# A state space layer's opening: two vectors spread over the partitions by TensorE, a shorter rotation, a written order for two engines

## The chip, the core and the metric

The kernel runs on one core of a Trainium2 chip as one program. The metric is the time of the whole program in device microseconds; lower is better. The core's engines are named as the profile names them: PE (TensorE, matmuls; PEld its weight loads), DVE (VectorE), ACT (ScalarE), POOL (GpSimd) and SP (SyncE, which here only issues DMAs).

## What is computed

Two layers of a trunk on a sequence of 512 tokens of width 1024. The first is a diagonal complex state space layer and a feed-forward layer, the second an attention layer and a feed-forward layer. The change lies in the state space layer alone:

```
h = rmsnorm(x, norm_mix[0])                      # gain of 1024 values
lam = complex(lam_re, lam_im)                    # 64 groups x 64 states
dt = exp(log_dt)[:, None]
a_bar = exp(lam * dt)
b_bar = ((a_bar - 1) / lam)[..., None] * complex(b_re, b_im)
bu = einsum('blgh,gph->blgp', h in groups of 16, b_bar)
states = associative_scan(a*, bu)                # over the 512 tokens
y = einsum('blgp,ghp->blgh', states, c).real + d_skip * h
y = gelu(y); val, gate = split(y @ w_glu); out = val * sigmoid(gate)
```

## The kernel before, in words

Everything named here is in `s5`. The 64 groups go in 8 units (`UN`) of 8 groups. Before the loop over the units there is an **opening** that prepares what all units share.

- Loads, all from SP's queue in the order written: `lam`, `ldt`, `braw` (the two parts of b), `xc` (the tokens, 8 loads of 256 KB), `gb`, `craw` (c) and `Dd`. `gb` (L418) is the norm gain, 1024 values, read once for each of 128 partitions. `Dd` (L425) is the skip vector, read for 32 partitions. Behind them come the weights of the GLU, `w_raw` (L262), through a pool of two buffers: a third `w_raw` is not issued before `w_lo` of the first has been computed.
- `wblock` splits each weight block in two: ACT copies `w_raw` to `w_hi` (L263), DVE subtracts to get `w_lo` (L265).
- ACT squares the tokens (`junk`, L457) and sums each row into `ss`. DVE scales `ss` (L491), POOL raises it to the power -1/2 (`rj`, L493). ACT multiplies the tokens by `rj` into `xn` (`normal`, L579; 32 copies for all eight columns), PE transposes them, ACT copies them to `U` (`tokens`, L596).
- b is transposed by PE, copied by ACT (L465), multiplied by `gb` in halves of 64 partitions by DVE (L468), then summed and subtracted (`Bs`, `Bd`, L494 and L495).
- `dt`, its exponential and cosine and sine are chains of DVE instructions on 128x32 elements (`Small`). `input_powers` builds the powers of the input side (`qt`, `qs`); `rotation` squares a phase eight times (`ephr`, `ephi`). `braid` writes the two alternately.
- `tables(u)` builds the table `W` of a unit (five DVE instructions), `turned` transposes it (`WT`, copied by ACT), `lags` and `chunk_inputs` are matmuls with it. `turn_factors` doubles the table `FG` three times with the phases (L699 to L701); `turns(u)` makes `E` of it. `powers` and `output_powers` do the output side. `output_side_out` copies c twice (`Cst`, and swapped `Csw`, ACT L573).

In the loop a unit's `scan` gives `X` on DVE (L750), PE multiplies it (`outputs`, L777 and L778), ACT applies the GELU, and the result `y` feeds the GLU's matmuls (L272 to L274), which `filler` places between the units. After the loop come the rest of the GLU, the feed-forward layer and the attention layer.

No order is written by hand in the opening or the loop (`manual` is an empty stack). The framework's scheduler sets the order of each engine's instructions by its own estimates; each engine then runs its list in that order. DMAs on SP's queue use eight semaphores in turn, so one waits for the eighth before it.

## Time and profile before

| | us |
|---|---|
| three runs | 1294.7, 1295.48, 1298.88 |
| median | 1295.48 |
| the profiled execution | 1299.89 |
| its span in the profile | 1298.2 |

| engine | busy us | share |
|---|---|---|
| PE | 1223.8 | 94% |
| DVE | 769.0 | 59% |
| ACT | 541.9 | 42% |
| POOL | 150.5 | 12% |

The shares are means over stages of different kinds. In the page's 40 slices of 32.5 us, PE's digits begin 2 5 6 9 and stay at 9, with one 8, while DVE's begin 7 9 9 9 9: the opening and the first units are the only stretch in which PE is not full. The span and what lies around it (1.7 us) make the profiled execution's own time; it stands 4.4 us above the median of the three runs. Times in the trace count from the span's start. An instruction's duration in the timeline overlaps the next one's by about 0.1 us, so the distance from start to start is what an engine's list costs.

### The profile page before, as it was taken

The page shows a single profiled execution, that of the slowest core. Times are in us where ns is not written, and L with a number is a line of the kernel's source. Part 1 is how long each engine was busy: PE and PEld are TensorE (multiplying, and loading weights), DVE is VectorE, ACT ScalarE, POOL GpSimd, SP SyncE. Part 2 cuts the span into 40 slices and gives each one's busy share as a digit, 9 for nine tenths or more (in the row PEclk, how much of TensorE's full clock was granted, in tenths as well). Part 3 has the DMA queues.
Part 4 walks back from the last instruction along what each step waited for, and adds up shares of the span by engine and source line. Part 5 has one row for each costly group of instructions (what it writes and reads, how often), then busy time and mean ns, then how long its engine had stood idle before and what let it go on. Part 6 is the DMA issues. An engine that isn't in the chain of part 4 may idle for free.

```text
span 1298.2 us, 17961 instructions
## 1 busy us (share of the span) xinstructions
PE 1223.8 (94%) x6796; PEld 1048.7 (81%) x6796; DVE 769.0 (59%) x1546; ACT 541.9 (42%) x1224; POOL 150.5 (12%) x177
## 2 busy tenths in 40 slices
PE   2569999999999999999989799999999999999998
PEld 1457878888888888888989799998888888888887
DVE  7999958654444443335899977775754444443221
ACT  5645536433333322223563678875533333332221
POOL 2000000000000000005744354520000000000000
PEclk9979999999999999999999899999999999999999
DMA  5101223333333333332213111111333333333341
GB/s 139 54 19 52 71 84 114 104 98 97 97 98 98 98 92 99 94 105 71 92 52 98 49 50 34 42 30 53 106 112 95 96 96 95 97 93 101 108 118 46
DMA packets 189894, 108.65 MB, mean 84 GB/s; under 512 B 7224, under 2 KB 188560, under 8 KB 189744
## 3 DMA queue, kind: packets, MB, share of 16 engines
q1 hardware_dynamic: 189424, 107.35, 28.4%
q8 instruction: 53, 0.87, 0.3%
q14 instruction: 33, 0.27, 0.1%
q10 hardware_dynamic: 384, 0.16, 0.1%
HBM read 103.04 MB, written 2.10 MB: 81 GB/s over the span
## 4 chain that ended last, share of the span: by engine, by line
PE 75%; DVE 8%; ACT 1%; issue 1%; DMA 0%; POOL 0%; ACTq 0%; DVEq 0%; POOLq 0%
PE acc L272 21%; PE acc L273 21%; PE acc L274 21%; PE acc L1026 7%; PE acc L1231 2%; DVE mask L1134 2%; DVE m L1133 2%; PE tr L1220 1%; DVE mask L1121 1%; PE lg L1204 1%; DVE pe L1207 1%; PE lg L1203 1%; PE tr L1063 0%; DVE kl L1081 0%; ACT pe L1210 0%
## 5 line engine op out<-in xcount | busy, mean ns | idle before, releaser
L263 ACT ACTIVATE w_hi<-w_raw 128x1024 fp32r<-128x1024 f32 (+5 forms) x208 | 199.9, 963 | 508.2 <-PE acc L273 461.1
L265 DVE TENSOR_TENSOR w_lo<-w_raw,w_hi 128x1024 fp32r<-128x1024 f32 (+6 forms) x179 | 194.2, 1085 | 146.5 <-ACT w_hi L263 145.4
L272 PE MATMUL acc<-h,w_hi 128*128 128x512 f32 x704 | 274.5, 390 | 0.0
L274 PE MATMUL acc<-h,w_lo 128*128 128x512 f32 x704 | 273.9, 389 | 0.0
L273 PE MATMUL acc<-h,w_hi 128*128 128x512 f32 x704 | 273.7, 389 | 0.0
L1026 PE MATMUL acc<-w_hi,h 128*128 128x256 f32 (+1 forms) x896 | 175.6, 293 | 0.8 <-ACT h L284 0.8
L272 PEld LDWEIGHTS acc<-h,w_hi 128*128 128x128 f32 x704 | 132.1, 188 | 28.0 <-issue 0.5
L274 PEld LDWEIGHTS acc<-h,w_lo 128*128 128x128 f32 x704 | 132.1, 188 | 27.6
L273 PEld LDWEIGHTS acc<-h,w_hi 128*128 128x128 f32 x704 | 132.1, 188 | 27.5 <-issue 0.5
L1026 PEld LDWEIGHTS acc<-w_hi,h 128*128 128x128 f32 x896 | 142.1, 193 | 1.4 <-ACT h L284 1.0
L1026 PE MATMUL acc<-w_lo,h 128*128 128x256 f32 (+1 forms) x448 | 127.3, 289 | 0.3 <-POOL w_lo L267 0.3
L339 DVE TENSOR_TENSOR u<-acc,rinv 128x512 f32<-128x512 f32 x44 | 30.4, 691 | 132.4 <-PE acc L274 132.4
L272 PE MATMUL acc<-f,w_hi 128*128 128x512 f32 x272 | 106.4, 391 | 0.0
L274 PE MATMUL acc<-f,w_lo 128*128 128x512 f32 x272 | 105.9, 389 | 0.0
L273 PE MATMUL acc<-f,w_hi 128*128 128x512 f32 x272 | 105.8, 389 | 0.0
L1026 PEld LDWEIGHTS acc<-w_lo,h 128*128 128x128 f32 x448 | 85.5, 193 | 0.8 <-POOL w_lo L267 0.5
L336 DVE TENSOR_TENSOR g<-acc,rinv 128x512 f32<-128x512 f32 x44 | 30.4, 691 | 85.3 <-PE acc L274 85.1
L267 POOL TENSOR_TENSOR w_lo<-w_raw,w_hi 128x1024 fp32r<-128x1024 f32 (+2 forms) x29 | 69.5, 2407 | 47.6 <-ACT w_hi L263 46.8
L274 PEld LDWEIGHTS acc<-f,w_lo 128*128 128x128 f32 x272 | 51.0, 188 | 10.8
L273 PEld LDWEIGHTS acc<-f,w_hi 128*128 128x128 f32 x272 | 51.1, 188 | 10.4
L272 PEld LDWEIGHTS acc<-f,w_hi 128*128 128x128 f32 x272 | 51.1, 188 | 10.4
L272 PE MATMUL acc<-y,w_hi 128*128 128x512 f32 x128 | 51.9, 414 | 1.7 <-ACT y L796 1.1
(288 smaller groups left out, 1979.4 us busy)
## 6 DMA issues: line engine op xcount, KB each, us to landing
w_raw<-in_ffn_w_gate_up_dram SPq DMA_DIRECT2D x88, 512.0 KB, 3.7
w_raw<-in_ffn_w_down_dram SPq DMA_DIRECT2D x32, 448.0 KB, 3.5
w_raw<-in_dsa_w_in_dram SPq DMA_DIRECT2D x26, 512.0 KB, 3.4
w_raw<-in_ffn_w_down_dram SPq DMA_DIRECT2D x16, 512.0 KB, 3.7
w_raw<-in_dsa_w_o_dram SPq DMA_DIRECT2D x16, 256.0 KB, 2.9
w_raw<-in_s_w_glu_dram SPq DMA_DIRECT2D x6, 384.0 KB, 3.3
xc<-in_x_dram SPq DMA_DIRECT2D x8, 256.0 KB, 8.9
xr<-in_x_dram SPq DMA_DIRECT2D x4, 512.0 KB, 3.7
```

Source lines behind the costliest of these rows:

```text
L263: nc.scalar.activation(hi, raw, AF.Copy)
L265: nc.vector.tensor_tensor(lo, raw, hi, op=ALU.subtract)
L267: lo_engine.tensor_tensor(lo, raw, hi, op=ALU.subtract)
L272: mm(out, lhsT=whi, rhs=xx[:, 0], start=start, stop=False)
L273: mm(out, lhsT=whi, rhs=xx[:, 1], start=False, stop=False)
L274: mm(out, lhsT=wlo, rhs=xx[:, 0], start=False, stop=stop)
L336: nc.vector.tensor_tensor(g, ps[0], rinv, op=ALU.mult)
L339: nc.vector.tensor_tensor(u, ps[1], rinv, op=ALU.mult)
L1026: PE.matmul(pt[:, :n], lhsT=h[k][:, l, ts], rhs=ww, start=(k == 0 and i == 0), stop=(k == KT - 1 and i == 2))
L1133: V.max(m8, sc)
L1134: V.match_replace(out=sc, in_to_replace=m8, in_values=sc, imm_value=GONE)
L1231: PE.matmul(po[s, b][:, i * HD : (i + 1) * HD], lhsT=pT[:, j * P : (j + 1) * P], rhs=vv[j][:, (s * 4 + i) * HD : (s * 4 + i + 1) * HD], st ...
```

## The change

Four things change, all in `s5`.

1. **Gain and skip.** `gd`, 8 partitions x 128, holds both vectors (two loads of 4 KB, L414 and L415). `sel`, made by POOL, holds eight selection matrices. PE spreads the gain over the partitions by 16 matmuls (`pgb`), and ACT copies it to `gb`, now 128x512 with each half of the partitions holding its own groups. DVE multiplies skip and gain on 8 partitions (L466), PE spreads the product in 8 matmuls, and ACT copies it to `Dd` in two pieces. The two broadcast loads go, and so does DVE's product on 32x1024. The products with b read the transposes in PSUM directly, on all 128 partitions at once: two DVE instructions and no ACT copy, instead of four and two.
2. **The rotation's layout.** `ephr` and `ephi` are laid out so that `turn_factors` handles both of its parts in one instruction; its first doubling becomes two ACT copies.
3. **A written order.** From `sgn` to the end of the opening the DVE and ACT instructions that are written there keep the order of the code (`manual_schedule`). Instructions written later, in the loop, may still be placed between them; POOL, PE and SP are not bound.
4. **The order of the code.** `dt` moves ahead of the products with b, `Bs` and `Bd` right behind them. Only eight steps of `rotation` are braided with `input_powers`; the rest comes behind the first table. `turn_factors`, `turns` and `powers` move behind the first `lags`, `chunk_inputs`, the copies of c and the tokens.

```
+        gd = self.scratch(1, [KT, 2, P], "gd")
+        nc.sync.dma_start(out=gd[:, 0], in_=gain_row.rearrange("(k p) -> k p", p=P))
+        nc.sync.dma_start(out=gd[:, 1], in_=d_ap.rearrange("(k p) -> k p", p=P))
...
-        nc.sync.dma_start(out=gb.rearrange("p a b c -> p (a b c)"),
-                          in_=gain_row.rearrange("(o d) -> o d", o=1).to_broadcast([P, D]))
...
-        nc.sync.dma_start(out=Dd[DR:], in_=d_ap.rearrange("(o d) -> o d", o=1).to_broadcast([32, D]))
+        sel = self.scratch(0, [KT, KT, SP], "sel")
+        PL.memset(sel, 1.0)
+        PL.affine_select(out=sel, in_=sel, compare_op=ALU.is_equal, fill=0.0, base=0,
+                         pattern=[[-1, KT], [0, SP]], channel_multiplier=1)
+        manual.enter_context(tc.manual_schedule(engines={E_.DVE, E_.Activation}))
...
+        for q in range(KT):
+            for g2 in range(2):
+                PE.matmul(pgb[g2 * SP : (g2 + 1) * SP, q * SP : (q + 1) * SP], lhsT=sel[:, q], rhs=gv[:, :, g2],
+                          start=True, stop=True)
+        AC.activation(gb.rearrange("p a b -> p (a b)"), pgb, AF.Copy)
+        V.tensor_tensor(gd[:, 1], gd[:, 1], gd[:, 0], op=ALU.mult)
+        for half in range(2):
+            pd = self.acc()
+            for q in range(KT // 2):
+                PE.matmul(pd[SP:, q * P : (q + 1) * P], lhsT=sel[:, half * (KT // 2) + q], rhs=gd[:, 1],
+                          start=True, stop=True)
+            AC.activation(Dd[DR:, half * S : (half + 1) * S], pd[DR:], AF.Copy)
...
-            AC.activation(t, pb.rearrange("p (h g) -> p g h", h=H16), AF.Copy)
-            for g2 in range(2):
-                hs = slice(g2 * SP, (g2 + 1) * SP)
-                V.tensor_tensor(t[hs], t[hs], gb[hs, :, g2], op=ALU.mult)
+            V.tensor_tensor(t, pb.rearrange("p (h g) -> p g h", h=H16), gb, op=ALU.mult)
+        V.tensor_tensor(Bs, Br, bi, op=ALU.add)
+        V.tensor_tensor(Bd, bi, Br, op=ALU.subtract)
...
-        braid(input_powers(), rotation())
+        rot = rotation()
+        braid(input_powers(), (next(rot, None) for _ in range(8)))
...
-            for i in range(3):
+            F = FG.rearrange("p j w g n -> p j (w g) n")
+            AC.activation(F[:, 0, :, 1], ephr[:, 0].rearrange("p w g -> p (w g)"), AF.Copy)
+            AC.activation(F[:, 1, :, 1], ephi[:, 0, 1].rearrange("p w g -> p (w g)"), AF.Copy)
+            for i in range(1, 3):
...
+                V.tensor_tensor(f1, F[:, :, :, :n], mr, op=ALU.mult)
+                V.tensor_tensor(f2, F[:, ::-1, :, :n], mi, op=ALU.mult)
+                V.tensor_tensor(F[:, :, :, n : 2 * n], f1, f2, op=ALU.add)
...
+        normal(0)
         for q in range(2):
             output_side_out(q, pc[q], Cst, False)
-        normal(0)
         tokens(0)
         spread(0)
         W = {0: tables(0)}
-        turn_factors()
-        E = {0: turns(0)}
-        powers()
-        V.tensor_tensor(Dd[DR:], Dd[DR:], gb[DR:].rearrange("p a b c -> p (a b c)"), op=ALU.mult)
-        warm_up("w")
         WT = turned(W[0])
         pk = lags(0, W[0])
         S4 = {0: chunk_inputs(0, WT)}
-        ES = {0: turns_out(0, E[0])}
-        output_powers()
+        normal(1)
         for q in range(2):
             output_side_out(q, pc[q], Csw, True)
-        W[1] = tables(1)
+        for _ in rot:
+            pass
+        turn_factors()
+        E = {0: turns(0)}
+        ES = {0: turns_out(0, E[0])}
+        powers()
+        output_powers()
         lags_out(0, pk)
-        VV = readout(0)
-        normal(1)
         tokens(1)
         spread(1)
         normal(2)
+        W[1] = tables(1)
+        VV = readout(0)
+        manual.close()
```

How the engines' lists come out at three places follows. On ACT, behind the squares of the tokens, the list before was this (`Cz` and `RT` are small tables of the first unit):

```order
L457 ACTIVATE junk,ss<-xc_117 128x1024
L579 ACTIVATE xn_376<-xc_114,rj 128x8x16
...
L666 ACTIVATE Cz_140<-Cst 64x4x16 x4
L579 ACTIVATE xn_377<-xc_116,rj 128x8x16
L579 ACTIVATE xn_377<-xc_117,rj 128x8x16
L724 ACTIVATE RT<-r_106 128x4x63
L263 ACTIVATE w_hi<-w_raw 128x512
L263 ACTIVATE w_hi<-w_raw 128x768
```

And in the changed kernel, at the same place:

```order
L479 ACTIVATE junk,ss<-xc_117 128x1024
L263 ACTIVATE w_hi<-w_raw 128x512
L263 ACTIVATE w_hi<-w_raw 128x768 x2
L599 ACTIVATE xn_392<-xc_114,rj 128x8x16
L599 ACTIVATE xn_392<-xc_115,rj 128x8x16
```

The three `w_hi` copies of the GLU's first weights, of which two came behind 20 of the `xn` copies and the third behind all 32, now stand ahead of all of them.

On DVE in the changed kernel the matching `w_lo` subtractions stand inside the chain of small instructions (`sm`, `ks`, `cs`) that leads to the first power and to `ss`; this is the third of them:

```order
L122 SCALAR_TENSOR_TENSOR ks<-sm_295,sm_283 128x32
L122 SCALAR_TENSOR_TENSOR sm_298<-sm_298,sm_292 128x32
L265 TENSOR_TENSOR w_lo<-w_raw,w_hi 128x768
L115 TENSOR_SCALAR ks<-sm_298 128x32
L115 TENSOR_SCALAR sm_277<-sm_301 128x32
```

The first two `w_lo` stand 22 and 15 rows ahead of the third; before, all three came behind the first table `W`. Behind the third the list goes on for 15 rows to the scaling of `ss`, and for 45 more to the end of the first `W`.

The third place is ACT's list around the first column of `FG` in the changed kernel:

```order
L668 ACTIVATE WT<-tr 128x512 x2
...
L599 ACTIVATE xn_392<-xc_117,rj 128x8x16
L593 ACTIVATE Csw<-acc_394,sgn 64x512 x2
L593 ACTIVATE Csw<-acc_399,sgn 64x512 x2
L712 ACTIVATE FG<-ephr 128x64
L713 ACTIVATE FG<-ephi 128x64
```

and DVE's list where that column is read:

```order
L659 TENSOR_TENSOR W<-k_426,k_431 128x512
L122 SCALAR_TENSOR_TENSOR ephi<-ephr,ephi 128x32
...
L721 TENSOR_TENSOR f_502<-FG,ephr 128x128x2
L722 TENSOR_TENSOR f_503<-FG,ephi 128x128x2
L723 TENSOR_TENSOR FG<-f_502,f_503 128x128x2
```

Between the first `xn` copy and the first `FG` copy ACT's list holds 27 more `xn` copies, eight copies of c, four of `U`, four of `Cz`, one of `RT` and two of `WT`. Between the end of the first `W` and its first reading of `FG`, DVE's list holds 17 rows of the rotation. Before, `FG`'s first column came from DVE itself.

## Rows read from the trace of the kernel before

**Rows 1.** Two stretches of 20 us: length, busy us (and instructions) of each engine, TensorE's granted clock, DMA share, GB/s.

```profile
60.00:80.00 20.00, 13.71 (x119) 11.68 (x118) 19.51 (x38) 8.34 (x22) 0.12 (x1) 0.83 0.07 16
...
140.00:160.00 20.00, 20.00 (x157) 16.59 (x155) 19.35 (x35) 10.15 (x19) 0.11 (x1) 1.00 0.27 79
```

**Rows 2.** Timeline of the opening up to `rj`: start, duration, engine, line, operation, count, and in brackets the idle time before it and who ended it.

```profile
12.77 1.39 DVE L468 TENSOR_TENSOR hB<-hB,gb 64x512 f32<-64x512 f32 x2 [3.52 <-DMA gb<-in_norm_mix_dram]
...
14.36 1.38 DVE L468 TENSOR_TENSOR bi<-bi,gb 64x512 f32<-64x512 f32 x2
...
18.82 1.06 ACT L457 ACTIVATE junk<-xc 128x1024 f32<-128x1024 f32 x1 [1.15 <-DMA xc<-in_x_dram]
...
20.00 0.17 DVE L491 TENSOR_SCALAR ss<-ss 128x4 f32<-128x4 f32 x1 [0.96 <-ACT junk L457]
...
20.25 1.09 POOL L493 TENSOR_TENSOR rj<-ss,mhalf 128x4 f32<-128x4 f32 x1 [14.94 <-DVE sm L100]
```

**Rows 3.** The DMA view of the first 30 us: busy tenths in 40 slices of 0.75 us, the sum of the bytes, and two loads with their KB and us from issue to landing.

```profile
DMA  0001769999889999999999995797720000000000
...
DMA packets 3873, 4.51 MB, mean 150 GB/s; under 512 B 2408, under 2 KB 3136, under 8 KB 3808
...
gb<-in_norm_mix_dram SPq DMA_DIRECT2D x1, 512.0 KB, 8.2
w_raw<-in_s_w_glu_dram SPq DMA_DIRECT2D x1, 384.0 KB, 4.3
```

**Rows 4.** The tile `w_raw` in the first 60 us: line, engine, operation, count, duration in ns (least, median, most), first and last start; and the time of its loads from issue to landing.

```profile
L263 ACT ACTIVATE w_hi<-w_raw x3: 613/827/845, 37.2 to 46.0; 128x768 fp32r<-128x768 f32 x2, 128x512 fp32r<-128x512 f32 x1
L265 DVE TENSOR_TENSOR w_lo<-w_raw,w_hi x3: 691/946/951, 37.8 to 48.4; 128x768 fp32r<-128x768 f32 x2, 128x512 fp32r<-128x512 f32 x1
...
DMA to landing us min/median/max: 3.0/3.7/4.3
```

**Rows 5.** ACT's timeline from 20 to 48 us.

```profile
21.38 5.07 ACT L579 ACTIVATE xn<-xc,rj 128x128 f32<-128x128 f32 x17 [1.42 <-POOL rj L493]
26.36 1.37 ACT L573 ACTIVATE Cst<-acc,sgn 64x512 f32<-64x512 f32 x2
...
30.26 1.54 ACT L596 ACTIVATE U<-tr 64x256 f32<-64x256 f32 x4
...
36.87 0.40 ACT L724 ACTIVATE RT<-r 128x252 f32<-128x252 f32 x1
...
41.76 0.60 ACT L648 ACTIVATE WT<-tr 128x512 f32<-128x512 f32 x1
...
46.78 1.04 ACT L666 ACTIVATE Cz<-Cst 64x64 f32<-64x64 f32 x4
```

**Rows 6.** DVE's timeline: two small instructions, the last of the first `W` and the one behind it, and `FG` from its first instruction to the first of `turns`.

```profile
27.30 0.17 DVE L117 TENSOR_SCALAR ephr<-sm 128x32 f32<-128x32 f32 x1
27.39 0.18 DVE L100 TENSOR_TENSOR sm<-ephi 128x32 f32<-128x32 f32 x1
...
36.07 0.68 DVE L639 TENSOR_TENSOR W<-k,k 128x512 f32<-128x512 f32 x1
36.67 0.21 DVE L606 TENSOR_TENSOR t<-pwt,pow 128x64 f32<-128x64 f32 x1
...
38.42 0.27 DVE L699 TENSOR_TENSOR f<-FG,ephr 128x64 f32<-128x64 f32 x1
...
44.09 0.42 DVE L712 TENSOR_TENSOR e<-FG 128x256 f32<-128x256 f32 x1
```

**Rows 7.** `X` of the first two units on DVE, and PE's first instruction on the second one.

```profile
60.21 1.71 DVE L750 TENSOR_TENSOR X<-z,z 64x252 f32<-64x252 f32 x4
...
80.00 1.71 DVE L750 TENSOR_TENSOR X<-z,z 64x252 f32<-64x252 f32 x4
...
81.41 0.40 PE L778 MATMUL acc<-VV,X 128*64 128x128 f32 x2 [1.11 <-DVE X L750]
```

**Rows 8.** TensorE's clock: four stretches of 4 us, columns as in rows 1.

```profile
68.00:72.00 4.00, 0.00 (x0) 0.00 (x0) 3.97 (x10) 1.54 (x4) 0.00 (x0) 0.79 0.19 42
72.00:76.00 4.00, 3.36 (x25) 2.70 (x26) 4.00 (x7) 1.19 (x3) 0.12 (x1) 0.50 0.13 34
...
88.00:92.00 4.00, 4.00 (x18) 3.30 (x18) 4.00 (x8) 1.71 (x2) 0.11 (x1) 0.50 0.02 4
92.00:96.00 4.00, 4.00 (x46) 3.24 (x44) 4.00 (x7) 1.81 (x5) 0.00 (x0) 0.72 0.00 0
```

**Rows 9.** PE's timeline: the same four transposes twice, then what PE waited for behind the second unit's `X`.

```profile
57.88 0.63 PE L647 MATMUL tr<-ident,W 128*128 128x128 f32 x4 [1.18 <-DVE W L639]
...
72.64 1.12 PE L647 MATMUL tr<-ident,W 128*128 128x128 f32 x4 [5.29 <-ACT WT L648]
...
86.50 0.65 PE L777 MATMUL acc<-M,U 128*64 128x128 f32 x4 [1.85 <-DMA M<-Kd]
87.80 1.11 PE L791 MATMUL tr<-ident,yg 64*128 64x64 f32 x8 [0.65 <-ACT yg L783]
```

**Rows 10.** POOL's selection on `Dd`, a DVE instruction beside it, and DVE's product of `Dd` and the gain.

```profile
21.52 1.57 POOL L497 TENSOR_SCALAR_AFFINE_SELECT Dd<-Dd 32x1024 f32<-32x1024 f32 x1 [0.17 <-DMA Dd<-in_s_d_dram]
...
21.64 1.46 DVE L100 TENSOR_TENSOR sq<-sm,sm 128x32 f32<-128x32 f32 x1
...
25.25 1.22 DVE L874 TENSOR_TENSOR Dd<-Dd,gb 32x1024 f32<-32x1024 f32 x1
```

More of the change, by code (lines that the diff above doesn't have):

```diff
@@ L394, in s5 @@
         qs = sp.tile([P, T8, GP], F32, name="qs")
-        ephr = self.scratch(6, [P, 6, GP], "ephr")
-        ephi = self.scratch(5, [P, 6, 2, GP], "ephi")
+        ephr = self.scratch(6, [P, 3, 2, GP], "ephr")
+        ephi = self.scratch(5, [P, 3, 2, 2, GP], "ephi")
         FG = sp.tile([P, 2, 2, GP, 8], F32, name="FG")
@@ L411, in load_x @@
                 nc.sync.dma_start(out=xc[j][e * NCH : (e + 1) * NCH], in_=xv[e, :, j])
-        gb = self.slot("a13", [P, GP, 2, H16], "gb")
+        gd = self.scratch(1, [KT, 2, P], "gd")
+        nc.sync.dma_start(out=gd[:, 0], in_=gain_row.rearrange("(k p) -> k p", p=P))
+        nc.sync.dma_start(out=gd[:, 1], in_=d_ap.rearrange("(k p) -> k p", p=P))
+        gb = self.slot("a13", [P, GP, H16], "gb")
         craw = self.slot("b2", [P, 8, 2, SP], "craw")
@@ L450, in s5 @@
         V.tensor_copy(prm.rearrange("p a b -> p (a b)"), pp[:, : 3 * GP])
+        pgb = self.lg()
+        gv = gd[:, 0].rearrange("k (g g2 h) -> k g g2 h", g2=2, h=H16)
+        for q in range(KT):
[10 more added lines that the diff above has]
+            AC.activation(Dd[DR:, half * S : (half + 1) * S], pd[DR:], AF.Copy)
         ss = sp.tile([P, T8 // 2], F32, name="ss")
@@ L457, in square_tokens @@
             AC.activation(junk, xc[j], AF.Square, accum_out=ss[:, j : j + 1])
+        sm = Small(V, sp, [P, GP], "sm")
+        st2 = [P, 2, GP]
+        lr, li = prm[:, 0], prm[:, 1]
+        ln = sp.tile(st2, F32, name="ln")
+        dt = sm.exp(prm[:, 2])
         bi = self.scratch(2, [P, GP, H16], "bi")
@@ L464, in s5 @@
             square_tokens(i)
-            AC.activation(t, pb.rearrange("p (h g) -> p g h", h=H16), AF.Copy)
-            for g2 in range(2):
-                hs = slice(g2 * SP, (g2 + 1) * SP)
-                V.tensor_tensor(t[hs], t[hs], gb[hs, :, g2], op=ALU.mult)
+            V.tensor_tensor(t, pb.rearrange("p (h g) -> p g h", h=H16), gb, op=ALU.mult)
+        V.tensor_tensor(Bs, Br, bi, op=ALU.add)
+        V.tensor_tensor(Bd, bi, Br, op=ALU.subtract)
         square_tokens(2)
         square_tokens(3)
-        sm = Small(V, sp, [P, GP], "sm")
-        st2 = [P, 2, GP]
-        lr, li = prm[:, 0], prm[:, 1]
-        ln = sp.tile(st2, F32, name="ln")
-        dt = sm.exp(prm[:, 2])
         V.tensor_copy(ln[:, 0], li)
@@ L493, in s5 @@
         PL.tensor_tensor(rj, ss, self.mhalf[:, : T8 // 2], op=ALU.pow)
-        V.tensor_tensor(Bs, Br, bi, op=ALU.add)
-        V.tensor_tensor(Bd, bi, Br, op=ALU.subtract)
         dv = Dd[DR:].rearrange("p (g h) -> p g h", h=H16)
@@ L549, in rotation @@
                 s2 = sm.mul(si, si, sq[i % 2])
-                o = (ephr[:, lv], ephi[:, lv, 1]) if lv >= 0 else cc[i]
+                o = (ephr[:, lv % 3, lv // 3], ephi[:, lv % 3, 1, lv // 3]) if lv >= 0 else cc[i]
                 sm.stt(co, 2.0, si, ALU.mult, ALU.mult, o[1])
@@ L555, in rotation @@
                 if lv >= 0:
-                    sm.stt(co, -2.0, si, ALU.mult, ALU.mult, ephi[:, lv, 0])
+                    sm.stt(co, -2.0, si, ALU.mult, ALU.mult, ephi[:, lv % 3, 0, lv // 3])
                 if i < 3:
@@ L690, in turn_factors @@
             PL.memset(FG[:, 1, :, :, 0:1], 0.0)
-            for i in range(3):
+            F = FG.rearrange("p j w g n -> p j (w g) n")
+            AC.activation(F[:, 0, :, 1], ephr[:, 0].rearrange("p w g -> p (w g)"), AF.Copy)
+            AC.activation(F[:, 1, :, 1], ephi[:, 0, 1].rearrange("p w g -> p (w g)"), AF.Copy)
+            for i in range(1, 3):
                 n = 1 << i
-                sh = [P, 2, GP, n]
-                f1 = self.scratch(0, [P, 2, 2, GP, 4], "f1")[:, :, :, :, :n]
-                f2 = self.scratch(1, [P, 2, 2, GP, 4], "f2")[:, :, :, :, :n]
-                mr = ephr[:, i::3].unsqueeze(3).to_broadcast(sh)
-                for j in range(2):
-                    mi = ephi[:, i::3, j].unsqueeze(3).to_broadcast(sh)
-                    V.tensor_tensor(f1[:, j], FG[:, j, :, :, :n], mr, op=ALU.mult)
-                    V.tensor_tensor(f2[:, j], FG[:, 1 - j, :, :, :n], mi, op=ALU.mult)
-                    V.tensor_tensor(FG[:, j, :, :, n : 2 * n], f1[:, j], f2[:, j], op=ALU.add)
+                sh = [P, 2, 2 * GP, n]
+                f1 = self.scratch(0, [P, 2, 2 * GP, 4], "f1")[:, :, :, :n]
+                f2 = self.scratch(1, [P, 2, 2 * GP, 4], "f2")[:, :, :, :n]
+                mr = ephr[:, i].rearrange("p w g -> p (w g)").unsqueeze(1).unsqueeze(3).to_broadcast(sh)
+                mi = ephi[:, i].rearrange("p j w g -> p j (w g)").unsqueeze(3).to_broadcast(sh)
+                V.tensor_tensor(f1, F[:, :, :, :n], mr, op=ALU.mult)
+                V.tensor_tensor(f2, F[:, ::-1, :, :n], mi, op=ALU.mult)
+                V.tensor_tensor(F[:, :, :, n : 2 * n], f1, f2, op=ALU.add)
         def turns(u):
@@ L924, in s5 @@
             filler(GLU_BLOCKS[u] * u - sum(f))
-        manual.close()
         xr = []
```

## The prediction

> **What bounds the kernel now.** The page first: TensorE is busy 94% of the span, and its slices are short of full only at the start, so a gain or a loss of this change must show up as an earlier or later start of full TensorE work. The stretches say where that start is: from 60 to 80 us VectorE works 19.51 of 20 us and TensorE 13.71; from 140 to 160 TensorE works all 20 [rows 1]. Then the hand-over: the first unit's `X` ends at 60.21 + 1.71 = 61.9, the second's at 80.00 + 1.71 = 81.7, and TensorE stood idle for `X` of the second unit, 1.11 us [rows 7]. Behind that point TensorE hardly waits. So VectorE's list up to the second `X` sets the end, and I price the change at that instruction. What comes later is the same work in nearly the same order, and I take it to move by the same amount.
>
> Within VectorE's list the reader is to see three things: it stood 3.52 us for the broadcast gain at the start, it had the token sums at 20.00 and `rj` was ready at 21.3 [rows 2], and from the first table on it ran almost without a gap.
>
> **What the change takes off VectorE.** The products with b were two pairs of 1.39 and 1.38 us [rows 2]; two full-width ones at 0.6 each, the distance from 36.07 to 36.67 [rows 6], make 1.2: 1.6 us less. The product on `Dd`, 1.22 us [rows 10], becomes a small one of 0.1. `FG` took 38.42 to 44.09 [rows 6], 5.7 us, 1.0 of which is other work placed there (one `w_lo` and a sum of the powers); two doublings in six instructions at 0.33 (0.42 less the overlap) and 0.6 make 2.8: 1.9 us less. Together 4.6 us of VectorE's work. The new matmuls (24 small ones) and the two copies to `Dd` lie in the first 12 us, beside transfers that nothing can overtake; if that cover were gone they would cost the second product with b, some 2 us, but behind it VectorE then waits anyway (next part). `Dd`'s selection on POOL stretched one VectorE instruction to 1.46 us before [rows 10]; now it starts when `Dd` is copied, near 12 us, where VectorE waits for the second transpose, so I count that 1.3 us as gone too.
>
> **What the new order puts in: the first wait.** The transfers ran from about 2.2 to 22.5 us with 4.51 MB [rows 3], 0.223 MB a us. Without the two broadcasts (0.66 MB) they end 2.9 us earlier; the two small loads ahead of b push everything by 0.9 (two issues at 0.46). So the last tokens, at 18.82 before [rows 2], come at 17.4 (only the gain's 2.35 us were ahead of them), and the two first GLU weights at 18.7 and 20.5. ScalarE squares the last tokens until 18.5, and then its list asks for these weights: `w_hi` 18.7 to 19.3 (0.61), `w_lo` on VectorE to 20.0 (0.69) [rows 4]. VectorE, with the products done near 15.1 and 17 small instructions at 0.09 [rows 6], has been there since 16.7: a wait of 2.6 us. Second block: `w_hi` 20.5 to 21.3, a wait of 0.7, `w_lo` to 22.3. The third block's load needs the first's buffer, so it starts at 20.0; loads take 3.0 to 4.3 us [rows 4], I take 3.6, between the ends, since the queue is nearly empty by then; `w_hi` to 24.4, `w_lo` to 25.4. VectorE arrived at 23.7: 0.8 us of waiting. What is queued behind on VectorE is the whole chain to `ss`, so 15 small ones later `ss` is done at 27.2, not 20.2, and with 1.2 us for POOL's `rj` [rows 2] ScalarE starts `xn` at 28.4, not 21.38 [rows 5].
>
> **The second wait.** From `ss` VectorE needs 45 rows to the end of the first table, 8.5 us (36 small ones at 0.1 with some wider, then 0.34 and 0.6 apiece): 35.7, against 36.7 before. The 17 rows of rotation behind it bring it to 37.4, where it reads `FG`'s first column. That column now comes from ScalarE, behind everything from the first `xn` on: 28 `xn` at 0.298 (17 in 5.07) 8.3; eight copies of c at 0.685 5.5; `U` 1.54; `Cz` 1.04; `RT` 0.35; two `WT` 1.1 [rows 5]: 17.8 us. The trace has no copy of 128x64; the nearest rows are a quarter of the four `Cz` (0.26) and an `xn` (0.30), so two cost 0.4 to 0.6, and I take 0.4. The Trainium skill (ScalarE: Activation LUTs, "What ACT_TABLE_LOAD costs") gives 186 ns plus 0.833 ns an element for such a copy, 0.24 us: by it the sum would be the same to 0.1. The column is ready at 28.4 + 18.2 = 46.6. VectorE waits 9.2 us. Nobody's work can slip in there, since its list is fixed.
>
> **The sum.** From 46.6: `FG` 2.8, `turns` six at 0.33 2.0, three small copies and the first product of the scan 0.9, the powers 1.6, then `Kd`, the second table, the scan, the readout's first three, `turns` of the next unit and `X`: 12.2. The first `X` ends at 66.1. To the second one VectorE has 36 rows, 21.3 us at the same distances (before 19.8; the difference is three readout instructions that used to come earlier and a table instruction that came later). So the second `X` ends at 87.4 against 81.7: **5.7 us later**, the 13.3 us of waits less the work that is gone and the idle time that was there before. Against the profiled execution's 1299.9 that is 1305.6; against the median of the runs, 4.4 below it, 1301.2. The median is what I predict on.
>
> Bounds: if the transfers start no later and the third load takes 3.0, 1.5 us come off (+4.2). If dropping the broadcasts does not hasten the weights (they land at 21.8 as before) and the load takes 4.3, 3.8 come on (+9.5). The value nearest to the rows is the middle one.
>
> **Rivals.**
>
> *TensorE makes it up.* Behind the second `X` it waited 1.85 us for the lag matrices `M` and 0.65 for the GELU [rows 9], and from 88 to 96 its granted clock was 0.50 and then 0.72 [rows 8], which cost 2.0 + 1.1 us. If both waits and half of that loss do not come back, 4.1 of the 5.7 return: 1297.1, no change that can be told. It decides if `M` has landed and the clock is high when the second unit's outputs end. For it: full from there on. Against: `Kd`, which starts `M`, stands directly ahead of the second `X` in both lists, so `M` is as late after it as before. 14%.
>
> *A colder TensorE.* From 68 to 72 TensorE did nothing, then its granted clock was 0.50, 1.2 GHz, and four transposes took 1.12 us instead of 0.63 [rows 8, 9]. With VectorE waiting 9.2 us TensorE idles longer ahead of the first units' outputs; one more cold stretch like that from 88 to 96 costs 3.1 us where TensorE is the bound: 1304.3. The Trainium skill (TensorE: Matmul & The Clock Gate, "What's actually happening") says the low clock is the default and activity lifts it; the trace agrees with its 0.50 behind the empty stretch, and by that rule this rival's loss is likely, though the outputs are followed by the same work as before. For it: 5.29 us of idle time were enough. Against: before the second `X` TensorE has the same transposes and lags at the same distance as now. 19%.
>
> *It does what it says.* If the weights are there when VectorE asks and `FG`'s column is there when it is read, the 13.3 us of waits vanish and the second `X` comes 7.6 us earlier than now: 1287.9, faster. It decides if ScalarE reaches the `FG` copies ahead of VectorE, which without the first waits is there at 33.3, that is if `rj` is ready by 15.1 and not 28.4. For it: 4.6 us of VectorE's work are really gone. Against: the last tokens alone are not there before 17, and their square, `ss` and `rj` take 2.5 more even without the weights between. 7%.
>
> **How the numbers follow.** My forecast, 1301.2, has 60%, with a range of its own from 1299.7 to 1305.0. The other three have 14, 19 and 7%. The range for 8 in 10 reaches down into the first rival, whose lower half and the last rival are left out (14%), and up to 1305.5, above both the cold rival and the upper bound: 1296.8 to 1305.5. A measurement of this kernel tells about 0.3%, 3.9 us, from no change, so faster means below 1291.6 and slower above 1299.4. Faster: the last rival, 7%. Slower: the forecast but for a twentieth (57) and the cold rival (19), 76%. Same: 17%.
>
> **What would show it.** In the trace of the changed kernel: VectorE idle 2 to 4 us ahead of the first `w_lo` near 19 us and a little ahead of the third; `ss` near 27; ScalarE's first `xn` near 28.4; one idle piece of VectorE of about 9 us ended by ScalarE's `FG` copy near 46.6; the first `X` near 66, the second near 87, and TensorE waiting for the second. If the weights land before 17 us the first wait is wrong. If the `FG` wait is under 5 us, the price of ScalarE's list is wrong. If the second `X` is 5 to 6 us late but the end is not, the rival of TensorE making it up holds.

## The result and the profile after

The changed kernel takes 1308.95 us (median of four runs, 1307.28 to 1310.98), the kernel before 1296.26 us (four runs, 1294.7 to 1298.88). The ratio is 1.0097, with a 95% interval from 1.0073 to 1.012: slower by 12.7 us, where 5.7 were forecast. Every ratio below is to executions of the kernel before that were taken beside the run, whose medians lie between 1295.91 and 1296.95 us.

The page of the changed kernel, its total busy time and the 40 slices of TensorE and VectorE:

```profile
span 1305.6 us, 18053 instructions
PE 1231.9 (94%) x6844; PEld 1053.7 (81%) x6844; DVE 765.1 (59%) x1532; ACT 544.1 (42%) x1227; POOL 152.0 (12%) x179
PE   3379999999999999999989899999999999999998
DVE  6799976754444443334799977675654444442221
```

VectorE has 3.9 us less to do than before (769.0), and the kernel is later all the same. The dip near the middle of PE's digits (8 9 8) lies in the kernel before too (8 9 7, of which the text above names only the 8), far behind the layer that changed. The stretches, in the same form as [rows 1] (engine busy time and count, then granted clock, DMA share and GB/s):

```profile
40.00:60.00 20.00, 6.99 (x55) 6.57 (x56) 11.63 (x32) 12.76 (x36) 0.11 (x1) 0.82 0.03 6
60.00:80.00 20.00, 13.82 (x91) 11.44 (x89) 19.88 (x41) 10.15 (x29) 0.00 (x0) 0.67 0.06 14
140.00:160.00 20.00, 20.00 (x127) 16.17 (x127) 19.53 (x38) 8.70 (x20) 0.11 (x1) 1.00 0.21 59
```

From 60 us on the picture is that of [rows 1]; between 40 and 60 VectorE, the engine on whose list the layer hangs, works 11.6 of 20 us. Its timeline, with what it waited for in brackets, at the two products with b, the weight splits, `ss`, and the turn column (the first column of `FG` that has to be computed):

```profile
10.57 0.69 DVE L492 TENSOR_TENSOR hB<-tr,gb 128x512 f32<-128x512 f32 x1 [1.28 <-ACT gb L465]
15.25 0.69 DVE L492 TENSOR_TENSOR bi<-tr,gb 128x512 f32<-128x512 f32 x1 [3.99 <-PE tr L490]
...
19.99 0.69 DVE L265 TENSOR_TENSOR w_lo<-w_raw,w_hi 128x512 fp32r<-128x512 f32 x1 [0.94 <-ACT w_hi L263]
...
21.29 0.96 DVE L265 TENSOR_TENSOR w_lo<-w_raw,w_hi 128x768 fp32r<-128x768 f32 x1
...
24.62 0.96 DVE L265 TENSOR_TENSOR w_lo<-w_raw,w_hi 128x768 fp32r<-128x768 f32 x1 [0.85 <-ACT w_hi L263]
...
27.98 0.16 DVE L512 TENSOR_SCALAR ss<-ss 128x4 f32<-128x4 f32 x1
...
39.35 0.18 DVE L122 SCALAR_TENSOR_TENSOR ephi<-ephr,ephi 128x32 f32<-128x32 f32 x1
48.03 0.42 DVE L721 TENSOR_TENSOR f<-FG,ephr 128x256 f32<-128x256 f32 x1 [8.49 <-ACT FG L713]
```

In place of the 3.52 us for the broadcast gain [rows 2] stand 1.28 and 3.99 us at the two products, 1.8 at the splits, and 8.49 at the turn column. ScalarE's timeline shows who made VectorE wait:

```profile
19.33 0.63 ACT L263 ACTIVATE w_hi<-w_raw 128x512 fp32r<-128x512 f32 x1 [0.68 <-DMA w_raw<-in_s_w_glu_dram]
20.42 0.84 ACT L263 ACTIVATE w_hi<-w_raw 128x768 fp32r<-128x768 f32 x1 [0.46 <-DMA w_raw<-in_s_w_glu_dram]
23.74 0.84 ACT L263 ACTIVATE w_hi<-w_raw 128x768 fp32r<-128x768 f32 x1 [2.48 <-DMA w_raw<-in_s_w_glu_dram]
29.42 1.27 ACT L599 ACTIVATE xn<-xc,rj 128x128 f32<-128x128 f32 x4 [4.84 <-POOL rj L514]
...
44.88 2.77 ACT L593 ACTIVATE Csw<-acc,sgn 64x512 f32<-64x512 f32 x4
47.55 0.31 ACT L712 ACTIVATE FG<-ephr 128x64 f32<-128x64 f32 x1
47.69 0.31 ACT L713 ACTIVATE FG<-ephi 128x64 f32<-128x64 f32 x1
```

`xn` starts at 29.42 (21.38 in [rows 5]), and the two copies that VectorE stands waiting for, whose last inputs are among its rotation rows that end at 39.5, come behind the whole list, at 47.55. The ends of `X` in VectorE's timeline, and the first transposes of `W` for the second unit in TensorE's:

```profile
67.16 1.71 DVE L772 TENSOR_TENSOR X<-z,z 64x252 f32<-64x252 f32 x4
90.16 1.71 DVE L772 TENSOR_TENSOR X<-z,z 64x252 f32<-64x252 f32 x4
```

```profile
59.46 1.09 PE L667 MATMUL tr<-ident,W 128*128 128x128 f32 x4 [9.74 <-DVE W L656]
```

The first `X` ends at 68.9 and the second at 91.9, 7.0 and 10.2 us later than in [rows 7].

A second trace of each kernel (the first two runs below) says how far single executions may be compared. The table gives, for all runs, VectorE's idle time ahead of the second `X` (its end less the busy time of that stretch), the end of the last transpose of the tokens with which the layer closes, and the time.

| kernel | first X | second X | idle before it | layer ends | from second X | median, us |
|---|---|---|---|---|---|---|
| before, first trace | 61.9 | 81.7 | 10.2 | 203.5 | 121.8 | 1296.26 |
| before again | 61.7 | 81.1 | 9.7 | 200.8 | 119.8 | 1295.84 (one) |
| changed | 68.9 | 91.9 | 22.0 | 211.9 | 120.0 | 1308.95 |
| changed again | 69.1 | 92.1 | 22.3 | 211.8 | 119.6 | 1308.91 |
| first wait out | 64.8 | 86.6 | 19.0 | 209.1 | 122.5 | 1306.52 |
| column by VectorE | 62.9 | 84.1 | 14.6 | 206.0 | 121.9 | 1303.89 |
| neither wait | 58.6 | 80.7 | 12.7 | 204.2 | 123.5 | 1300.03 |
| neither, small rows first | 54.5 | 77.3 | 7.6 | 200.4 | 123.1 | 1296.92 |
| no fixed order | 59.9 | 77.0 | 9.2 | 196.6 | 119.6 | 1292.67 |
| splits of three later | 58.8 | 92.6 | 22.7 | 216.0 | 123.4 | 1312.3 |
| column and three later | 52.5 | 85.8 | 16.2 | 206.5 | 120.7 | 1302.47 |
| column and two later | 52.5 | 84.1 | 13.9 | 203.8 | 119.7 | 1300.25 |
| VectorE fixed only | 63.0 | 82.7 | 13.7 | 205.8 | 123.1 | 1301.35 |
| ScalarE fixed only | 59.8 | 79.6 | 13.2 | 204.5 | 124.8 | 1302.24 |
| old order, fixed | 62.7 | 86.1 | 16.8 | 208.6 | 122.5 | 1304.81 |
| spread only | 58.8 | 76.8 | 8.4 | 200.9 | 124.1 | 1297.75 |
| rotation only | 59.2 | 80.2 | 7.8 | 199.3 | 119.1 | 1296.74 |
| both, old order, free | 59.6 | 76.7 | 8.9 | 196.7 | 120.0 | 1292.74 |

Behind the layer the traces agree: span less layer end is 1093.2 to 1095.6 us in all eighteen. So the loss lies in this layer, and in the changed kernel the traces show nearly all of it at the second `X`.

### The profile page after: what moved, and what is told of

It reads as the page before. It is cut to its first block, busy times and chain, and to the rows that moved or that the text cites. A ratio compares the mean times of both kernels' runs of the same rounds, so it can differ in the third digit from the quotient of the medians.

```text
span 1305.6 us, 18053 instructions
## 1 busy us (share of the span) xinstructions
PE 1231.9 (94%) x6844; PEld 1053.7 (81%) x6844; DVE 765.1 (59%) x1532; ACT 544.1 (42%) x1227; POOL 152.0 (12%) x179
## 4 chain that ended last, share of the span: by engine, by line
PE 84%; DVE 7%; ACT 4%; DMA 2%; issue 1%; SPq 1%; POOL 0%; ACTq 0%; DVEq 0%; POOLq 0%
PE acc L272 22%; PE acc L273 22%; PE acc L274 22%; PE acc L1048 8%; PE acc L1253 2%; PE tr L1242 1%; PE tr L696 1%; DMA w_raw<-in_s_w_glu_dram 1%; PE acc L800 1%; PE acc L799 1%; DVE ro L985 1%; ACT xn L599 1%; PE lg L1226 1%; DVE pe L1229 1%; PE lg L1225 0%
```

## The experiments

**The two kernels once more.**

> The kernel before, once more, for its trace. In the six traces so far the time behind the last transpose of the opening layer is the same within 2 us (1093.6 to 1095.6 us to the end of the span), and the profiled execution of before was 3.6 us above its median. Theory: the place of that 3.6 us is the opening layer, so this trace shows the last transpose near 200 us (203.5 in the first trace) if its time is near the median of 1296.3 us. Rival: the 3.6 us lie behind the layer, and the last transpose is at 203 to 204 us again.

> The changed kernel once more, for a second trace and more times. Theory: the waits are the same in every execution (FG 8 to 9 us, the splits 6 us), the second X at 91 to 93 us; the last transpose of the layer at 211 to 214 us, and the time 1307 to 1311 us. Rival: the shift of the second X differs by more than 3 us between executions, and the loss is partly chance.

The kernel before took 1295.84 us, and its last transposes stand at

```profile
200.25 0.60 PE L937 MATMUL tr<-ident,xr 128*128 128x128 f32 x4
```

so 2.6 us of the 3.6 by which the first trace was slow lie in the layer, 2.0 of them behind the second `X`. The changed kernel repeated itself: 1308.91 us (ratio 1.0108, 1.0092 to 1.0123), the column waited for 8.5 us again, the layer's end is the same to 0.2 us. Against the second trace of before, the second `X` is 10.8 to 11.1 us late and the layer's end 11.0. The loss is no accident of an execution; that it looked like 8.4 us at the end of the layer in the first pair of traces came from the slower execution in the first trace of before.

**The turn column by VectorE.**

```
-            AC.activation(F[:, 0, :, 1], ephr[:, 0].rearrange("p w g -> p (w g)"), AF.Copy)
-            AC.activation(F[:, 1, :, 1], ephi[:, 0, 1].rearrange("p w g -> p (w g)"), AF.Copy)
+            V.tensor_copy(F[:, 0, :, 1], ephr[:, 0].rearrange("p w g -> p (w g)"))
+            V.tensor_copy(F[:, 1, :, 1], ephi[:, 0, 1].rearrange("p w g -> p (w g)"))
```

> The changed kernel, but the first doubling of FG (L712, L713) is copied by VectorE and not by ScalarE; the order of everything else stays. Theory: VectorE's wait of 8.5 us for these two copies, which stood at the end of ScalarE's list, made most of the loss. It vanishes, the first unit's X ends near 60.8 us (68.9 in the changed kernel), the second's near 84, and the time is 1300 to 1303 us (the changed kernel: 1308.95). Rival: ScalarE's list is late anyway (Csw for the readout, the ES copies and the output powers come behind the same normalised tokens), so VectorE waits a few rows later for the same list; X of the first unit stays within 2 us of 68.9 and the time is 1307 to 1309 us.

1303.89 us (ratio to before 1.0058, 1.0046 to 1.007). VectorE's timeline at the place of the 8.49 us:

```profile
39.75 0.22 DVE L712 COPY FG<-ephr 128x64 f32<-128x64 f32 x1
39.85 0.22 DVE L713 COPY FG<-ephi 128x64 f32<-128x64 f32 x1
40.10 0.43 DVE L721 TENSOR_TENSOR f<-FG,ephr 128x256 f32<-128x256 f32 x1
```

The wait is gone for 0.4 us of VectorE's work, the second `X` comes 7.8 us earlier and the time falls by 5.1, to just above the 1300 to 1303 expected. The rival, that VectorE meets the same list some rows later, falls: 2.0 us at the first product of the scan (for TensorE's `lg`) is all that is left of it.

**The splits later.** Three runs ask for the first weight blocks at a written place, so that they can no longer float up ahead of `ss`.

```
         lags_out(0, pk)
+        refill(3)
         tokens(1)
```

> The changed kernel, but the first three GLU weight blocks are asked for behind lags_out(0), inside the fixed order, so their splits (w_hi by ScalarE, w_lo by VectorE) no longer float up ahead of the token norms. Theory: with the splits goes the wait that held the norm's rj (ScalarE began xn at 29.4 us, at 21.4 before the change); xn starts 5 to 7 us earlier, the turn column by ScalarE comes 5 to 7 us earlier too and VectorE's wait for it stays about 8 us long; since VectorE still makes the splits (2.6 us) before the first X, X ends 3 to 5 us earlier, and the time is 1304 to 1306 us. Rival: the splits were only filling a wait that is there anyway (VectorE waits for ScalarE's turn column in either case until the same moment); xn moves, X does not, 1308 to 1310 us.

With the vector copy as well:

> The changed kernel with both edits: the turn column copied by VectorE, and the first weight splits behind lags_out(0). Theory: the two waits together are the whole loss, and VectorE has some 4 us less work than in the kernel before; the first X ends at 56 to 59 us (61.9 before the change), the second's at 78 to 81 us (81.7), and the time is 1294 to 1298 us. Rival: a third thing holds it (a TensorE at the low clock in the loop's first two units, the order in the loop), and the time stays at 1300 us or above though no long wait is left on VectorE.

With the vector copy and `refill(2)` at that place:

> The changed kernel with the turn column copied by VectorE and two (not three) weight blocks asked for behind lags_out(0), so no split waits for a third load, which takes a buffer that the first split must free: in the run with three ScalarE stood 5.2 us and VectorE 3.3 us for it between the first and the second X. Theory: that wait was what was left of the loss there; the second X ends at 80 to 83 us (85.8 with three) and the time is 1296 to 1299.5 us (1302.47 with three). Rival: the second X is late because the readout's and the second table's rows (some 8 us of VectorE) stand behind the first X and not ahead of it: 1300 to 1303 us.

1312.3 us (1.013, 1.0114 to 1.0146), 1302.47 (1.0054, 1.0041 to 1.0067) and 1300.25 (1.003, 1.002 to 1.004). All three missed what the theory expected. The first missed in sign: `X` of the first unit did come 10 us earlier, but the second later than in the changed kernel. The second stayed above the 1294 to 1298 us expected. In the second run, ScalarE and VectorE between the two `X`:

```profile
57.09 0.84 ACT L263 ACTIVATE w_hi<-w_raw 128x768 fp32r<-128x768 f32 x1 [5.17 <-DMA w_raw<-in_s_w_glu_dram]
```

```profile
57.96 0.96 DVE L265 TENSOR_TENSOR w_lo<-w_raw,w_hi 128x768 fp32r<-128x768 f32 x1 [3.27 <-ACT w_hi L263]
58.84 0.68 DVE L654 TENSOR_TENSOR k<-hB,qs 128x512 f32<-128x512 f32 x1
```

There are two buffers for raw weights; the third block can be loaded only when the first has been split, and by writing the split into the fixed order I had put that load's whole latency in front of the second table and the readout (L654 and on). A moved row is only as good as what it needs there. With two blocks the wait is gone, and so are 2.2 us. The second `X`, at 84.1, did not come down to the 80 to 83 expected, and the time is the rival's.

**Each wait by itself.** With the two splits as the last rows of the fixed order nothing is moved behind them.

```
         VV = readout(0)
+        refill(2)
         manual.close()
```

> The changed kernel with the two weight blocks as the last rows of the fixed order: only the first wait is out, the turn column is still copied by ScalarE behind its list. Theory: ss moves up by some 4 us (24 us in the runs with the splits later) and everything behind it too, the wait for FG stays 8 to 9 us, the second X ends near 88 us and the time is 1303.5 to 1306 us. Rival: as in the run with three splits later, the time does not fall, 1308 us or more, because something other than the slot of the third block made that run slow.

With the vector copy:

> The changed kernel with the turn column copied by VectorE and two weight blocks asked for as the last rows of the fixed order, so that neither of the two waits is there and no row of the second table or the readout is moved behind the splits. In all traces so far the second X follows VectorE's idle time ahead of it (10.2 us of idle in the kernel before, 22.0 in the changed one, 13.9 in the run with two splits later). Theory: the idle time is what counts, wherever the rows stand; it is 13 to 14 us here as well (4.0 us of it at the second B product, 2.2 and 1.5 at the start, 2 at the first scan), the second X ends at 82 to 84.5 us and the time is 1298 to 1300.5 us. Rival: it was the rows behind the first X that held the run with two splits later; then the second X comes below 81 us and the time is 1295 to 1297 us.

1306.52 us (1.0084, 1.007 to 1.0098) and 1300.03 (1.0032, 1.002 to 1.0043). So taking out the first wait alone (its splits move along with it) is worth 2.4 us, where 3 to 5.5 were expected, the second alone 5.1, both 8.9. Without both the kernel is still 3.9 us behind the kernel before. In the run without both the time was that of the theory; the second `X`, at 80.7, was the rival's, and behind it 123.5 us followed instead of some 120. That the second `X` and the end go together is true of the changed kernel, not of every order.

**A third wait.** VectorE's chains of small rows (`ln` to the first powers) are written ahead of the products with b:

```
+        V.tensor_copy(ln[:, 0], li)
...
+        V.scalar_tensor_tensor(pw[0][:, 1], er, -1.0, cs[:, 1], op0=ALU.mult, op1=ALU.mult)
         bi = self.scratch(2, [P, GP, H16], "bi")
         for i, t in ((0, Br), (1, bi)):
```

> As the run with neither wait, and VectorE's small rows (exponential, rotation start, first powers; 55 rows of 0.1 us) written ahead of the B products instead of behind them. Theory: a third wait of the fixed order is that of the B products, 1.4 and 4.0 us ahead of 15.25 us, with the small rows shut in behind it; in front of it they fill it, ss comes 3 to 4 us earlier (20 to 21 us), the second X ends at 79 to 81 us and the time is 1294 to 1297 us. Rival: ss has to wait for the last token square anyway and ScalarE's list then sets the pace: less than 1.5 us is gained.

1296.92 us (1.0008, 0.9998 to 1.0017): with these three edits the changed kernel, its order still fixed, is level with the kernel before. The products now wait for nothing, and `ss`, at 27.98 in the changed kernel and 23.94 with the two waits out, comes at

```profile
17.07 0.68 DVE L506 TENSOR_TENSOR hB<-tr,gb 128x512 f32<-128x512 f32 x1
17.67 0.68 DVE L506 TENSOR_TENSOR bi<-tr,gb 128x512 f32<-128x512 f32 x1
...
19.59 0.16 DVE L512 TENSOR_SCALAR ss<-ss 128x4 f32<-128x4 f32 x1
```

The 3.99 us at the second product were a cost of the order too: the small rows that could have filled them were written behind. But the order did not make the product late; TensorE's list did. In the changed kernel (first three lines) the selection matmuls stand ahead of the second transposes of b, which in the kernel before (last line) waited only for their load:

```profile
7.92 1.97 PE L463 MATMUL lg<-gd,sel 8*64 8x64 f32 x32
9.69 3.62 PE L470 MATMUL acc<-gd,sel 8*64 8x128 f32 x16
13.24 1.98 PE L490 MATMUL tr<-ident,braw 32*128 32x32 f32 x16
```

```profile
9.22 1.97 PE L463 MATMUL tr<-ident,braw 32*128 32x32 f32 x16 [1.66 <-DMA braw<-in_s_b_im_dram]
```

So the transposes come 4.0 us later than before, and the matmuls that spread the skip product, 3.6 us that nothing in the products with b reads, stand in front of them. Whether the change does better with these behind the transposes was not tried. The run with the three edits is still 4.3 us behind the next one; what makes that difference was not tried either.

**Without the fixed order.**

```
-        manual.enter_context(tc.manual_schedule(engines={E_.DVE, E_.Activation}))
```

> The changed kernel without the fixed order of VectorE and ScalarE: the rows are written as there, but the scheduler may move them. Theory: the loss lies in what the fixed order makes VectorE wait for; free to fill the wait, the scheduler puts tables and powers ahead of the turn factors, the 8.5 us wait shrinks below 3 us and the time is 1298 to 1303 us. Rival: the loss is in the written order and the early weight splits themselves, which stay, and the time is 1306 to 1310 us.

1292.67 us (0.9975, 0.9966 to 0.9983): faster than both kernels and than I expected. This one line is worth 16.3 us. ScalarE's and VectorE's timelines at the turn column:

```profile
33.47 0.32 ACT L711 ACTIVATE FG<-ephr 128x64 f32<-128x64 f32 x1
33.63 0.30 ACT L712 ACTIVATE FG<-ephi 128x64 f32<-128x64 f32 x1
34.22 3.33 ACT L598 ACTIVATE xn<-xc,rj 128x128 f32<-128x128 f32 x11
```

```profile
31.44 0.68 DVE L658 TENSOR_TENSOR W<-k,k 128x512 f32<-128x512 f32 x1
33.96 0.42 DVE L720 TENSOR_TENSOR f<-FG,ephr 128x256 f32<-128x256 f32 x1 [1.57 <-ACT FG L712]
```

The scheduler puts the copies ahead of the later tokens, 14 us earlier than in the changed kernel, and only one split ahead of the tables. For one engine alone:

```
-        manual.enter_context(tc.manual_schedule(engines={E_.DVE, E_.Activation}))
+        manual.enter_context(tc.manual_schedule(engines={E_.DVE}))
```

> The changed kernel with only VectorE in fixed order; ScalarE is ordered by the scheduler. Theory: the loss is made by ScalarE's fixed list, at whose end the turn column stands, and by the splits that slip in ahead of the norm; with ScalarE free its copies come when they are ready, but VectorE's splits still stand in its row (two of three ahead of ss), so half is left: 1298 to 1304 us. Rival: VectorE's own fixed row is the cause, and the time stays at 1305 us or more.

and with `{E_.Activation}`:

> The changed kernel with only ScalarE in fixed order; VectorE is ordered by the scheduler, which puts the splits behind ss. Theory: the turn column still stands at the end of ScalarE's list, but VectorE fills the wait with other rows (powers, the second table), so the wait for FG is under 5 us and the first X ends 2 to 4 us earlier than in the changed kernel: 1302 to 1306 us. Rival: the chain through ScalarE's list to FG, turns and the scan sets the time whatever VectorE does beside it: 1307 to 1310 us.

1301.35 us (1.004, 1.0026 to 1.0054) and 1302.24 (1.0046, 1.0033 to 1.0059). Either engine held alone costs 8.7 to 9.6 us over none held, and together 16.3: the loss is not one engine's. In both runs VectorE waits under a microsecond for the turn column. With VectorE alone held that is because ScalarE's copies come earlier. With ScalarE alone held the wait has in part only moved, to the row just ahead:

```profile
40.09 0.29 DVE L702 TENSOR_TENSOR Kd<-tr,Dd 128x128 f32<-128x128 f32 x1 [4.05 <-PE tr L696]
41.13 0.43 DVE L721 TENSOR_TENSOR f<-FG,ephr 128x256 f32<-128x256 f32 x1 [0.75 <-ACT FG L713]
```

TensorE's `tr` there had itself waited for `WT`, which ScalarE's held list copies at 35.71 us, behind `xn` copies and a `w_hi`.

**Fixing or rewriting?** Spread and rotation in the order in which the kernel before is written, free and held:

> The kernel before with spread and rotation, in the order in which the kernel before is written, and no fixed order. Theory: the whole loss of the change is in the fixed order, so this is as fast as the changed kernel without it (1292.67 us): 1291 to 1295 us. Rival: the rewritten order is what made that run fast, and this one is at 1295 to 1299 us.

> Spread and rotation in the order in which the kernel before is written (1292.74 us with the scheduler free), with VectorE and ScalarE held to that written order. Theory: it is the fixing that costs, not the rewriting: here too the first weight splits slip in ahead of the norm and wait for their loads, Csw comes late, and the time is 1300 us or more. Rival: the rewritten order is bad in itself when held, with its turn factors behind a long list of ScalarE; in the old order FG stands early in ScalarE's list and the time is within 3 us of 1292.7.

1292.74 us (0.9965, 0.9953 to 0.9977) and 1304.81 (1.0064, 1.0051 to 1.0077). Free, the two written orders cannot be told apart (1292.67 us at 0.9975 and 1292.74 at 0.9965); held, the old one costs 12.1 and the new one 16.3. So it is the holding that costs, whichever of the two orders is held; the rewriting adds 4 us to it. That is said of these two orders: with three groups of rows placed otherwise a held order was level with the kernel before. Held, the old order keeps the turn column off the wait, but the splits float up ahead of `ss` there too:

```profile
20.15 0.69 DVE L265 TENSOR_TENSOR w_lo<-w_raw,w_hi 128x512 fp32r<-128x512 f32 x1 [0.69 <-ACT w_hi L263]
22.43 0.96 DVE L265 TENSOR_TENSOR w_lo<-w_raw,w_hi 128x768 fp32r<-128x768 f32 x1 [0.97 <-ACT w_hi L263]
24.85 0.96 DVE L265 TENSOR_TENSOR w_lo<-w_raw,w_hi 128x768 fp32r<-128x768 f32 x1
29.62 0.16 DVE L509 TENSOR_SCALAR ss<-ss 128x4 f32<-128x4 f32 x1
```

**The two edits alone,** in the old order, free:

> The kernel before with one part of the change: norm weight and skip spread by TensorE, B products straight from PSUM; rotation and written order as before, no fixed order. Theory: the spread itself is a small gain, because VectorE's row loses the B and skip products (2.7 us) and the wait of 3.5 us for the broadcast weight: 1292 to 1296 us. Rival: the spread delays the B products (TensorE's rows now stand in front of the transposes, the first bi came at 15.25 us, 14.36 before) and pulls the weight splits up, and costs: 1298 to 1301 us.

> The kernel before with one part of the change: the new layout of the rotation factors, the first doubling of FG copied by ScalarE and six VectorE instructions for 18; spread and order as before. Theory: VectorE loses 1.9 us of work and, with the order free, its wait for ScalarE's copies stays under 2 us (1.6 us in the run without fixed order): 1294 to 1297 us. Rival: the copies by ScalarE hold VectorE also where the scheduler places them: 1298 us or more.

1297.75 us (1.0006, 0.9997 to 1.0015) and 1296.74 (0.9996, 0.9987 to 1.0005): each by itself changes nothing that can be told (the spread by itself missed the 1292 to 1296 us expected), together they gain 4.2 us over the kernel before beside them (1296.95). The spread does bring the second `X` from 81 to 76.8, as in the run with both, but 124.1 us follow: its sixth `X` ends 20.4 us behind the fifth, 17.3 with both. Which of the loop's rows does that was not tried.

## Why the prediction was wrong

The direction, the place and the mechanism were right; the size was not. The step that failed is the sum: it prices the rows of a held list at the distances that they have in a list filled by the scheduler, and has no wait for TensorE in it, so the second `X` was put at 87.4 and came at 91.9. By the prediction's own steps:

- **The second `X` sets the end.** Right for the changed kernel: 120.0 and 119.6 us follow it, 119.8 in the second trace of before. As a rule it fails: over all runs 119.1 to 124.8 us follow, a spread as wide as the forecast loss. "Behind that point TensorE hardly waits" was too strong, too: in the kernel before TensorE was busy 16 of 20 us there.

```profile
80.00:100.00 20.00, 16.02 (x117) 13.11 (x115) 19.76 (x41) 9.54 (x22) 0.11 (x1) 0.83 0.07 17
```

- **Work off VectorE: 4.6 us and 1.3 of stretched selection.** The rows bear most of it out. By the distance from start to start the `Dd` product went from 1.25 to 0.3, the products with b from 2.8 to 1.4 and the doublings from 4.7 to 3.3 (forecast 2.8): 3.8 us, not 4.6. The stretched row went from 1.46 to 0.18. Yet VectorE's busy time to the second `X` fell only from 71.5 to 69.8. One table instruction more stands ahead (0.7), the first copy took 2.12 us (1.60 before), and rows that overlapped their neighbours no longer do (below).
- **First wait.** Forecast 2.6, 0.7 and 0.8 us; measured 0.94, 0 and 0.85, because VectorE got there at 19.0 and not at 16.7: the second product with b was done at 15.9 and the sums right behind it at 17.3, where the prediction has all of it done near 15.1. The last split ended at 25.6 (forecast 25.4). `ss` came at 27.98, not 27.2: the 14 rows between took 2.4 us, 0.17 apiece and not 0.1. `xn` started at 29.42, not 28.4. Taken out alone, with its splits, the wait is worth 2.4 us.
- **Second wait.** Forecast 9.2 us, until 46.6; measured 8.49, until 48.03; VectorE came there at 39.5, not 37.4, and so waited less although the column came later. ScalarE's list took 18.6 us from the first `xn`, forecast 18.2. The two copies at its end took 0.45 of it (0.4 was taken); one takes 0.31. By the Trainium skill (ScalarE: Activation LUTs, "What ACT_TABLE_LOAD costs": 186 ns plus 0.833 ns an element) the estimate for its size is 0.24; the measured 0.31 decides, and the difference is of no weight here. Taken out, the wait is worth 5.1 us.
- **The sum.** Here the prediction failed: 87.4 forecast, 91.9 measured. Of the 4.5 us, 1.0 is the chain to `xn`, 0.4 ScalarE's list, 1.3 VectorE's way from the column to the first `X` (20.8, forecast 19.5: the doublings took 3.3 for 2.8, the powers 2.2 for 1.6), 1.7 the way to the second (23.0, forecast 21.3; 1.4 of it a wait for TensorE's `tr` ahead of `Kd`, which no step had).

```profile
89.95 0.29 DVE L702 TENSOR_TENSOR Kd<-tr,Dd 128x128 f32<-128x128 f32 x1 [1.38 <-PE tr L696]
```

  No term is far off; all err to the same side. At 1.9 of the 4.5 us (the chain to `ss`, the doublings, the powers) the reason is that many rows now read the row just ahead of them, and such a row starts some 0.1 us later than one that doesn't (last section). The other 2.5 us up to the measured 12.7 are no step of the prediction. A second trace of before has its second `X` 0.6 us ahead of the first trace's; 0.6 more come behind the second `X`; and the profiled executions of the changed kernel (1307.28 and 1307.45 us) are each the fastest of their four, so that the traces show some 1.2 us less loss than the medians. Where these 1.2 us lie is open; the interval of the ratio reaches from 9.5 to 15.6 us.
- **What was left out.** The new matmuls were put at nothing (some 2 us at the worst), since VectorE "then waits anyway" behind the second product. They put its transposes 4.0 us later, and VectorE stood 3.99 us for them. With the first two waits there, that was hidden behind them as forecast; without them, moving the small rows into this third wait gave 3.1 us.
- **The rivals.** TensorE made nothing up that can be told. Its wait for `M` behind the second `X` did shrink, from 1.85 us [rows 9] to 0.78, and from 88 to 96 us its granted clock was 1.00; but 120.0 us follow the second `X`, as in the second trace of before (119.8), where that clock was 1.00 too. A colder TensorE is not needed either: from 50 to 70 us its granted clock was 0.64 and 0.50, but 0.59 and 0.55 in the second trace of before, at a normal time, and the cold stretch that this rival adds from 88 to 96 us is not there. "It does what it says" has its direction without the fixed order, 3.6 us faster than before, but not its price of 7.6.

## What to carry to other kernels

Try an order that is to be held with the scheduler free first: here the edits were a gain of 0.3%, the holding a loss of 1.3%. Where a list is held, look for every row whose input comes from another held list and ask what stands ahead of its producer there; a two-row copy at the end of a list of 18 us cost 5.1 us, more than the 3.8 us of rows that the change took off VectorE. And look at what still floats: rows that aren't held are put in between (here the weight splits, ahead of `ss` in both held orders), and a held list can't step around them. Ask the same of an engine that isn't held: new work for TensorE, small as it was, stood ahead of what VectorE needed next.

## What the runs showed of the hardware

- Small VectorE rows cost more when each reads the row ahead of it. In the changed kernel, in one chain of the exponential:

```profile
6.36 0.16 DVE L117 TENSOR_SCALAR sm<-prm 128x32 f32<-128x32 f32 x1
6.55 0.18 DVE L117 TENSOR_SCALAR sm<-sm 128x32 f32<-128x32 f32 x1
6.77 0.18 DVE L115 TENSOR_SCALAR sm<-sm 128x32 f32<-128x32 f32 x1
```

  They start 0.2 us apart; the mixed rows of [rows 6] start 0.1 apart at the same duration. Where two chains alternate (22.17 to 22.95 us in the same trace) the distance is 0.11, and in the rotation alone, which is written so that no row reads the row just ahead of it, the 17 rows from 37.70 to 39.35 start 0.10 apart.
- TensorE's granted clock falls at different places in executions of the same kernel. From 50 to 70 us it was 1.00 in the first trace of before (first two lines) and 0.59 and 0.55, between the two levels of 1.2 and 2.4 GHz, in the second (last two lines), which was the faster execution:

```profile
50.00:60.00 10.00, 4.85 (x50) 4.00 (x50) 10.00 (x19) 3.95 (x10) 0.00 (x0) 1.00 0.28 80
60.00:70.00 10.00, 6.35 (x56) 5.69 (x55) 9.81 (x22) 3.27 (x10) 0.00 (x0) 1.00 0.04 9
```

```profile
50.00:60.00 10.00, 5.33 (x40) 4.44 (x42) 10.00 (x20) 3.49 (x8) 0.00 (x0) 0.59 0.27 80
60.00:70.00 10.00, 9.73 (x57) 9.31 (x54) 9.81 (x22) 3.70 (x12) 0.00 (x0) 0.55 0.04 8
```
